# Feed-forward blocks of a two-layer diffusion trunk: every engine in emission order, as a pipeline of seven slots per unit

## The chip, the cores and the metric

The kernel runs on one core of a Trainium2 chip. The metric is the device time of one execution in microseconds (us). The kernel before has a median of 2194.66 us over three runs (2193.26 to 2200.68).

The engines of the core are PE (TensorE: matmuls, and beside them weight loads), DVE (VectorE), ACT (ScalarE), POOL (GpSimd) and SP (SyncE, which here only starts DMA transfers). Each engine executes its own instructions strictly in their order; an instruction that waits holds up all that stand behind it on the same engine.

## The reference, cut to what matters

The trunk has two layers. Each is a mixer (Hyena with mLSTM in layer 0, Mamba-2 in layer 1; neither is touched) and then a SwiGLU feed-forward block:

```python
for l in range(DEPTH):                                  # DEPTH = 2
    ...                                                 # the mixer
    x = x + g1 * out
    h = _rmsnorm(x, P['norm2_g'][l]) * (1 + sc2) + sh2
    ff = (jax.nn.silu(h @ P['ffn_w1'][l]) * (h @ P['ffn_w3'][l])) @ P['ffn_w2'][l]
    x = x + g2 * ff
```

`D_MODEL` is 1024 and the hidden width 2816, which is 22 tiles of 128. There are 640 tokens: 128 of context and 512 latent ones. All is fp32.

## The kernel before, in words

**Precision.** A matrix is split into a high part and the rest, both in the fast fp32 format: ACT copies the value into the rounded type (`split`, L462), and DVE, or POOL where the call says so, subtracts it from the value (L463). A product is three matmuls: high by high, high by low, low by high.

**Seven products.** In the feed-forward block two 128-row blocks of weights and the tokens in two halves of 320 (322 with two columns for shift) are multiplied as a 2x2 block product in the Strassen-Winograd form, with seven products in place of eight. The weights' seven operands are A11, A12 and A22, which are loaded, and S1 to S4, which are sums: S3 and S1 (L1868, L1869), and from these S2 and S4 (L1871, L1872). DVE writes the sums into one PSUM tile, `sw`, which serves both pairs in turn. So a unit's operands are prepared as: A11 and A12 split (`whi`, `wlo`); S3 and S1 formed and split (`wg` or `whif`, `wlof`); S2 and S4 formed over them and split; A22 split with POOL (`whie`, `wloe`).

**Units.** A *hidden tile* is one of the 22 tiles of the hidden width: seven products of 12 matmuls over K = 4 (`hidden`). Its products come into three PSUM banks, ACT copies them out (L1929), DVE adds (L1950, L1960, L1962) and POOL multiplies; ACT takes the SiLU in three pieces (L1970 to L1972) and DVE multiplies (L1973 to L1975). A *pair* is two of the eight tiles of the output, over six hidden tiles: seven products of 9 matmuls over K = 3 (`pair_block`). ACT copies out (L1893), DVE adds (L1907, L1910, L1912), and the result is scaled by the gate and added to `x`: by DVE in one instruction (`residual_part`, L2054), or for one of the four quarters by ACT (scale, L1914) and POOL (add, L1915).

**Order.** A layer's block is hidden tile 0; then three times six hidden tiles and four pairs; tiles 18 to 21 are multiplied by the rest of `w2` plainly (L1670 to L1675). The first hidden tile of the next group stands between a group's own last tile and its pairs. `hidden_quads` writes the hidden tiles, and the sums and splits that the pairs need of them.

**Buffers.** A unit loads two raw tiles of weights (`wraw`, L1422), `r1` with A11 and A12 and `r2` with A22 and the other. There are four buffers, so a unit's two loads wait until the unit two before it has read its own for the last time. `r1` is read last by L1872, `r2` by the split of A22.

**What sets the order on the engines.** The program is built in a context that simulates a timeline (`TileContext(schedule_with_timeline_sim=True)`): a scheduler with modelled durations decides in which order each engine gets its instructions. PE keeps the written order inside a unit.

Of the kernel before, what the change touches and what calls it, by code (L numbers as in the profile page):

```python
# [5 lines left out]
F32 = mybir.dt.float32  # L6
# [5 lines left out]
T = 640  # L12
# [257 lines left out]
class Kern:  # L270
# [1408 lines left out]
    def ffn(self, l, last):  # L1679
# [9 lines left out]
        with self.tc.tile_pool(name=f"hT{l}", **right) as hq, self.tc.tile_pool(name=f"fw{l}", **right) as wq:  # L1689
            with self.tc.tile_pool(name=f"ffn{l}", **right) as fp:  # L1690
                X = self.norm_quads(hq, fp, self.modA[l, 4], self.modA[l, 3], last)
                get2 = self.stream(self.I["w2"][l])
                steps = lambda j: self.hidden(fp, wq, self.I["w13"][l, j], X, j == 0, j % 2, (j + 2) % 3)

                def hid(j):
                    *_, h = steps(j)
                    return h
                h = hid(0)
                for c, (j0, j1) in enumerate(CHUNKS[:3]):
                    U, h = self.hidden_quads(fp, wq, hid, steps, j0, h)  # L1700
                    for e in range(4):
                        self.pair_block(fp, wq, self.I["w2q"][l, c, e], U, e, g2)
                uH, uL = [], []
                for j in range(18, 22):
                    h = h if j == 18 else hid(j)
                    H, L = [self.hb(x, j - 18) for x in "HL"]
                    for i, v in enumerate(h):
                        q = slice(320 * i, 320 * i + 320)
                        self.split(v[:, 2:322], H[:, q], L[:, q])
                    uH.append(H)  # L1710
                    uL.append(L)
# [89 lines left out]
    def hidden_quads(self, p, wq, hid, steps, j, ahead):  # L1801

        U = {}
        N = 320
        pool, sub = self.nc.gpsimd.tensor_tensor, ALU.subtract
        both = lambda v, n: v[:, 0:2 * n].rearrange("p (h n) -> p h n", n=n)[:, :, n - N:n]
        t4 = self.t(p, (128, 2 * N), "t4")

        def put(k, nms, v, dst, i=0):
            n = len(nms)
            dst = [d[:, N * i:N * (i + n)] for d in dst]
            self.split(both(v, 322) if n == 2 else v, *(both(d, N) if n == 2 else d for d in dst))
# [5 lines left out]
        for k in range(3):  # L1820
            a, b = hid(j + 2 * k) if k else ahead
            t1 = a[:, 324:644]
            pool(t1, b[:, 2:322], a[:, 2:322], op=sub)
            f = hb(3 * k) if k < 2 else fs(0)
            put(k, ("B11", "T1"), a, f)
            a2, b2 = hid(j + 2 * k + 1)
            b21, b22, t3, t2 = a2[:, 2:322], b2[:, 2:322], a2[:, 324:644], b2[:, 324:644]
            pool(t3, b22, b[:, 2:322], op=ALU.add)
            if k < 2:
                put(k, ("B21", "T3"), a2, us() if k else hb(1))  # L1830
            else:
                put(k, ("B21",), b21, f, 2)
            pool(t2, b22, t1, op=ALU.add)
            if k < 2:
                put(k, ("B22", "T2"), b2, us() if k else hb(2))
            t5 = t4[:, N * k:N * k + N] if k < 2 else b21
            pool(t5, b21, t2, op=sub)
        after = steps(j + 6)
        next(after)
        f = fs(1)  # L1840
        put(2, ("B22", "T2"), b2, f)
        put(2, ("T3",), t3, f, 2)
        g = [self.t(p, (128, 1024), "wg", WG, F32R) for _ in "HL"]
        self.split(t4, *(v[:, 0:2 * N] for v in g), self.nc.gpsimd)
        self.split(t5, *(v[:, 2 * N:3 * N] for v in g), self.nc.gpsimd)
        for i in range(3):
            U["T4", i] = tuple(v[:, N * i:N * i + N] for v in g)
        return U, next(after)

    def quad_parts(self, src, n, where, e):  # L1850

        nc = self.nc
        vec, sub = nc.vector.tensor_tensor, ALU.subtract
        r1, r2 = [self.raw_unit(src[i], 2 * n) for i in range(2)]
        W = {}

        def put(v, nms, pool, tag, bufs, eng=None):
            w = n * len(nms)
            h, lo = (self.t(pool, (128, 512 * len(nms)), *(("wg", WG) if tag == "g" else ("w" + x + tag, bufs)), F32R)
                     for x in ("hi", "lo"))  # L1860
            self.split(v, h[:, 0:w], lo[:, 0:w], eng)
            for i, nm in enumerate(nms):
                c = slice(n * i, n * i + n)
                W[nm] = h[:, c], lo[:, c]
        v = self.pp.tile([128, 1024], F32, name="sw", tag="sw", bufs=1)[:, 0:2 * n]
        put(r1, ("A11", "A12"), *where[0])
        a, b = slice(0, n), slice(n, 2 * n)
        vec(v[:, a], r2[:, b], r1[:, a], op=sub)  # L1868
        vec(v[:, b], r2[:, b], r2[:, a], op=sub)  # L1869
        put(v, ("S3", "S1"), *where[1])  # L1870
        vec(v[:, a], r1[:, a], v[:, b], op=sub)  # L1871
        vec(v[:, b], r1[:, b], v[:, a], op=sub)  # L1872
        put(v, ("S2", "S4"), *where[2])
        put(r2[:, a], ("A22",), *e, nc.gpsimd)
        return W

    def quad_product(self, W, X, K, i, P, first, ks=None):

        nc = self.nc
        a, b = (("A11", "B11"), ("A12", "B21"), ("S4", "B22"), ("S2", "T2"), ("S3", "T3"), ("S1", "T1"),  # L1880
                ("A22", "T4"))[i]
        for k in ks or range(K):
            h, lo = (v[:, 128 * k:128 * k + 128] for v in W[a])
            xh, xl = X[b, k]
            for j, (w, x) in enumerate(((h, xh), (h, xl), (lo, xh))):
                nc.tensor.matmul(P, w, x, start=first and k == j == 0, stop=k == K - 1 and j == 2,  # L1886
                                 skip_group_check=not first)

    def pair_block(self, p, wq, src, U, e, g):

        nc = self.nc
        n, N = 384, 320
        vec, add, copy = nc.vector.tensor_tensor, ALU.add, lambda o, v: nc.scalar.activation(o, v, AF.Copy)  # L1893
        two = [(p, "g", WG), (wq, "f2", 1)]
        W = self.quad_parts(src, n, ((self.wp, "", 2), two[e % 2], two[1 - e % 2]), (p, "e", 1))
        A, C, D = [self.ps("ab")[:, 0:N] for _ in range(3)]
        c11, c12, c22, _ = [v[:, 322 * i:322 * i + N] for v in [self.t(p, (128, 644), "nt1", 2) for _ in range(2)]
                            for i in range(2)]
        put = lambda i, P, *fl: self.quad_product(W, U, 3, i, P, *fl)
        put(0, A, True)  # L1900
        copy(c11, A)
        put(5, C, True)
        copy(c22, C)
        put(3, A, False)
# [170 lines left out]

# [8 lines left out]
```

## Time and profile before

| | |
|---|---|
| median of three runs | 2194.66 us (2193.26 to 2200.68) |
| the profiled execution: its own time | 2200.58 us |
| its span, first to last instruction | 2198.8 us |
| granted TensorE clock, mean | 0.97 of full speed |
| PE busy | 2056.4 us, 94% of the span |
| DVE busy | 1633.8 us, 74% |
| ACT busy | 1088.4 us, 49% |
| POOL busy | 719.0 us, 33% |

The two feed-forward blocks lie at about 601 to 1024 us and 1732 to 2156 us of the span. PE's busy share is over the whole span; what it leaves idle inside these blocks is read there, from windows and from single instructions.

### The profile page before, as it was taken

What the parts mean: (1) busy time and instruction counts of PE and PEld (TensorE: products, weight loads), DVE (VectorE), ACT (ScalarE), POOL (GpSimd) and SP (SyncE); (2) the same over time, 40 slices, a digit from 0 to 9 for tenths busy, and PEclk for the clock granted to TensorE, in tenths of its full rate; (3) what the DMA queues carried; (4) which work ended last, traced back from release to release, by engine and by line L of the source; (5) the groups of instructions that cost most, each with busy time, mean ns of one, the idle gap of its engine ahead of it and who ended that gap; (6) DMA issues with size and microseconds to landing.
All of it is one profiled execution on the core that took longest, in us unless ns stands there. A gap on an engine that the chain in (4) does not pass through costs nothing.

```text
span 2198.8 us, 35965 instructions
## 1 busy us (share of the span) xinstructions
PE 2056.4 (94%) x14034; PEld 1909.4 (87%) x14034; DVE 1633.8 (74%) x2709; ACT 1088.4 (49%) x1882; POOL 719.0 (33%) x725
## 2 busy tenths in 40 slices
PE   4899999999899999999889999999999899999997
PEld 2788798878799999999889899999988898989996
DVE  7775465678988888887687777776743988888895
ACT  3755634322554545554475556555512554545452
POOL 4311121234444252523332232323312353443422
PEclk9899999989899999999899999999999899999998
DMA  7544431674122222223312222222354122222231
GB/s 280 177 150 158 135 106 64 197 265 156 43 78 66 89 72 82 76 83 118 91 58 67 64 60 71 57 66 62 125 190 145 49 64 81 84 70 87 68 97 48
DMA packets 85638, 225.38 MB, mean 103 GB/s; under 512 B 9979, under 2 KB 27899, under 8 KB 85468
## 3 DMA queue, kind: packets, MB, share of 16 engines
q1 hardware_dynamic: 71756, 205.44, 28.9%
q10 hardware_dynamic: 8960, 9.86, 1.4%
q0 software_dynamic: 4752, 7.79, 1.3%
q8 instruction: 110, 1.80, 0.3%
q14 instruction: 60, 0.49, 0.1%
HBM read 204.86 MB, written 18.36 MB: 102 GB/s over the span
## 4 chain that ended last, share of the span: by engine, by line
PE 68%; DVE 19%; DMA 5%; ACT 3%; issue 3%; POOL 1%; SPq 0%; ACTq 0%; DVEq 0%; POOLq 0%
PE mm L1886 11%; PE aux L1886 9%; PE mm L1670 5%; PE mm L1672 5%; PE mm L1674 5%; PE mm L1671 3%; PE mm L1675 3%; PE mm L1673 3%; DMA wraw<-in_w 2%; DVE x L2054 2%; DVE wlof L463 2%; PE md L1498 2%; DVE wlo L463 1%; PE aux L1319 1%; ACT whi L462 1%
## 5 line engine op out<-in xcount | busy, mean ns | idle before, releaser
L462 ACT ACTIVATE whi<-wraw 128x1024 fp32r<-128x1024 f32 (+1 forms) x176 | 181.2, 1029 | 327.1 <-PE mm L1673 124.9
L1670 PE MATMUL mm<-hH,whi 128*128 128x384 f32 x760 | 267.6, 353 | 0.2 <-DVE x L2054 0.2
L1674 PE MATMUL mm<-hH,wlo 128*128 128x384 f32 x760 | 265.2, 349 | 0.9 <-DVE wlo L463 0.9
L1672 PE MATMUL mm<-hL,whi 128*128 128x384 f32 x760 | 265.0, 349 | 0.5 <-DVE hL L463 0.4
L463 DVE TENSOR_TENSOR wlo<-wraw,whi 128x1024 fp32r<-128x1024 f32 (+1 forms) x162 | 195.0, 1204 | 88.9 <-ACT whi L462 87.2
L1671 PE MATMUL mm<-hH,whi 128*128 128x258 f32 (+1 forms) x568 | 168.6, 297 | 7.4 <-DVE U L639 7.4
L1675 PE MATMUL mm<-hH,wlo 128*128 128x258 f32 (+1 forms) x568 | 167.9, 296 | 0.0
L1673 PE MATMUL mm<-hL,whi 128*128 128x258 f32 (+1 forms) x568 | 167.4, 295 | 0.0
L1670 PEld LDWEIGHTS mm<-hH,whi 128*128 128x128 f32 x760 | 145.0, 191 | 12.6 <-issue 9.3
L1674 PEld LDWEIGHTS mm<-hH,wlo 128*128 128x128 f32 x760 | 144.8, 190 | 5.0 <-issue 3.2
L1672 PEld LDWEIGHTS mm<-hL,whi 128*128 128x128 f32 x760 | 144.9, 191 | 3.8 <-issue 2.0
L1671 PEld LDWEIGHTS mm<-hH,whi 128*128 128x128 f32 x568 | 110.2, 194 | 11.3 <-issue 10.1
L463 POOL TENSOR_TENSOR wloe<-wraw,whie 128x512 fp32r<-128x512 f32 (+1 forms) x68 | 85.1, 1251 | 95.8 <-ACT whie L462 95.8
L1675 PEld LDWEIGHTS mm<-hH,wlo 128*128 128x128 f32 x568 | 109.7, 193 | 4.2 <-issue 3.2
L1673 PEld LDWEIGHTS mm<-hL,whi 128*128 128x128 f32 x568 | 110.2, 194 | 2.3 <-issue 1.3
L463 DVE TENSOR_TENSOR wlof<-sw,whif 128x1024 fp32r<-128x1024 f32 (+1 forms) x68 | 76.5, 1125 | 25.9 <-ACT whif L462 25.9
L1316 POOL TENSOR_TENSOR xw<-xB,ec 128x256 f32<-128x256 f32 x64 | 47.9, 753 | 127.8 <-PE aux L1319 78.3
L462 ACT ACTIVATE wg<-sw 128x1024 fp32r<-128x1024 f32 (+1 forms) x68 | 64.4, 947 | 42.9 <-PE mm L1886 19.5
L1963 POOL TENSOR_TENSOR nt<-nt,rb 128x322 f32<-128x322 f32 x44 | 44.4, 1008 | 125.4 <-DVE nt L1962 113.2
L463 DVE TENSOR_TENSOR wg<-sw,wg 128x1024 fp32r<-128x1024 f32 (+1 forms) x68 | 76.5, 1125 | 10.7 <-ACT wg L462 10.2
L462 ACT ACTIVATE whif<-sw 128x1024 fp32r<-128x1024 f32 (+1 forms) x68 | 64.5, 948 | 33.3 <-DVE sw L1872 29.1
L1366 POOL TENSOR_TENSOR it<-it 128x256 f32<-128x256 f32 x32 | 30.2, 943 | 100.0 <-DVE it L1364 100.0
(793 smaller groups left out, 7063.7 us busy)
## 6 DMA issues: line engine op xcount, KB each, us to landing
wraw<-in_w SPq DMA_DIRECT2D x96, 512.0 KB, 3.5
modr<-in_modw SPq DMA_DIRECT2D x56, 512.0 KB, 4.0
wraw<-in_odw SPq DMA_DIRECT2D x49, 512.0 KB, 3.5
wraw<-in_w2q SPq DMA_DIRECT2D x48, 384.0 KB, 3.1
wraw<-in_evw SPq DMA_DIRECT2D x25, 512.0 KB, 4.3
wraw<-in_modw SPq DMA_DIRECT2D x24, 512.0 KB, 3.8
wraw<-in_odow SPq DMA_DIRECT2D x16, 512.0 KB, 3.7
kd<-kst ACTq DMA_DIRECT2D x16, 256.0 KB, 3.2
```

Of the source, the lines that this page charges most:

```text
L462: self.nc.scalar.activation(h, src, AF.Copy)
L463: (eng or self.nc.vector).tensor_tensor(lo, src, h.bitcast(F32), op=ALU.subtract)
L1316: nc.gpsimd.tensor_tensor(xw, xB[c][:, 0:256].rearrange("p (h e) -> p h e", h=4), self.ec[:, c, hd[d]].unsqueeze(2).to_broadcast([128, 4, ...
L1498: nc.tensor.matmul(ps[32 * j:32 * j + 32, 0:256], self.scond[:, 32 * k:32 * k + 32], rs[0][:, 256 * j:256 * j + 256], start=k == 0, stop=k ...
L1670: nc.tensor.matmul(pA, h, rh[k][:, 0:384], start=f, stop=False)
L1671: nc.tensor.matmul(pB, h, rh[k][:, 384:T_], start=f, stop=False)
L1672: nc.tensor.matmul(pA, h, rl[k][:, 0:384], start=False, stop=False)
L1673: nc.tensor.matmul(pB, h, rl[k][:, 384:T_], start=False, stop=False)
L1674: nc.tensor.matmul(pA, lo, rh[k][:, 0:384], start=False, stop=l)
L1675: nc.tensor.matmul(pB, lo, rh[k][:, 384:T_], start=False, stop=l)
L1886: nc.tensor.matmul(P, w, x, start=first and k == j == 0, stop=k == K - 1 and j == 2, skip_group_check=not first)
L1963: pool(s0, s0, rb1, op=mul)
```

## The change

The seven products, the operands and all arithmetic stay. What changes is the order in which instructions are written, and who decides it:

- `run_units` lists a layer's units and writes them inside `tc.manual_schedule()`, in which every engine gets its instructions in the order in which they are written.
- A unit has seven slots. In slot n stand: its product number n (`SLOTS`, the same order as before); for n < 2 what is left of the unit before (`tail`); the reading of its product n-1 (`read`); steps of the *next* unit's operands (`EARLY` where both are hidden tiles, `LATE` where one is a pair); sums and splits of finished hidden tiles (`hidden_parts`); in slot 1 the split of its own A22; in slot 2 the two loads of the unit after the next.
- The residual addition of the quarter `c12` (`x[2e][:, 320:640]`) is moved from DVE to ACT and POOL, as `c22`'s was: 24 in all (4 pairs by 3 groups by 2 layers). DVE's list shrinks from 2670 to 2646, ACT's grows from 1883 to 1907 and POOL's from 709 to 733.
- Tags change in places: the first hidden tile after pairs has its sums in `f2` and `g` in that order, and a pair's two are swapped.

Its core (what is left out are the removed functions, which are printed above, and `products_first`, the first tile as before):

```diff
+    def run_units(self, l, p, wq, X, g):
...
+        units = [hid(0)]
+        for c in range(3):
+            units += [hid(6 * c + m) for m in range(1, 7)]
+            units += [PairBlock(self, p, wq, I["w2q"][l, c, e], U, e, g) for e in range(4)]
+        units += [hid(j) for j in (19, 20, 21)]
...
+        with self.tc.manual_schedule():
+            for i, u in enumerate(units):
+                prev = units[i - 1] if i else None
+                nxt = units[i + 1] if i + 1 < len(units) else None
+                late = nxt and not (u.hidden and nxt.hidden)
+                extra = self.hidden_parts(p, wq, units, i, U, T4, last)
+                for n, product in enumerate(SLOTS):
+                    if i:
+                        u.product(product)
+                    if n < 2 and prev:
+                        prev.tail(n)
+                    if i and n:
+                        u.read(n - 1)
+                    if nxt:
+                        for step in (EARLY, LATE)[late].get(n, ()):
+                            nxt.prep(step)
+                    for f in extra.get(n, ()):
+                        f()
+                    if i and n == 1:
+                        u.prep_own()
+                    if n == 2 and i + 2 < len(units):
+                        units[i + 2].load()
...
+SLOTS = (0, 5, 3, 2, 4, 1, 6)
+PREP = ("S31", "H31", "L31", "S24", "HA", "LA", "H24", "L24")
+EARLY = {0: ("S31",), 1: ("H31",), 2: ("HA", "L31", "S24"), 3: ("H24", "LA"), 4: ("L24",)}
+LATE = {0: ("S31",), 2: ("HA",), 3: ("LA",), 4: ("H31",), 5: ("L31", "S24"), 6: ("H24", "L24")}
...
+class PairBlock(Unit):
...
+        if n == 0:
...
+            copy(self.c11, self.A)
+        elif n == 1:
+            copy(self.c22, self.C)
+        elif n == 2:
+            copy(self.c12, self.A)
+        elif n in (3, 4):
+            c, d, bank = ((self.c12, 2 * self.e, self.C), (self.c22, 2 * self.e + 1, self.A))[n - 3]
+            vec(c, c, bank, op=ALU.add)
+            copy(c, c, scale=self.g[:, d, 1:2])
+            nc.gpsimd.tensor_tensor(k.x[d][:, N:T], k.x[d][:, N:T], c, op=ALU.add)
+        elif n == 5:
+            vec(self.c11, self.c11, self.D, op=ALU.add)
+            for a, b in ((0, 128), (128, N)):
+                k.residual_part(2 * self.e, self.c11, 0, a, b, self.g)
+    def tail(self, n):
+        if n == 0:
+            for a, b in ((0, 128), (128, self.N)):
+                self.k.residual_part(2 * self.e + 1, self.A, 0, a, b, self.g)
...
+class HiddenTile(Unit):
...
+        if n == 0:
+            self.tiles()
+            copy(self.s0, self.A)
+        elif n == 1:
+            copy(self.c22, self.C)
+        elif n == 2:
+            copy(self.s1, self.A)
...
+    def tail(self, n):
...
+        if n == 0:
+            if not self.first:
+                nc.vector.tensor_tensor(u3, self.A, self.rb1, op=mul)
+            nc.scalar.activation(s0[:, 2:130], s0[:, 2:130], AF.Silu, bias=s0[:, 0:1])
+            nc.scalar.activation(s0[:, 130:], s0[:, 130:], AF.Silu, bias=s0[:, 1:2])
+        else:
+            stt(s0[:, 2:130], u3[:, 2:130], u3[:, 0:1], s0[:, 2:130], op0=add, op1=mul)
+            stt(s0[:, 130:], u3[:, 130:], u3[:, 1:2], s0[:, 130:], op0=add, op1=mul)
```

The names of the steps: S31 forms S3 and S1, S24 forms S2 and S4; H and L are the two halves of a split (ACT copy, DVE subtraction), of A11 and A12 (HA, LA), of S3 and S1 (H31, L31) and of S2 and S4 (H24, L24).

**DVE, inside a group's pairs.** Before, around the end of pair 0; `sw_7279` is the sum tile of pair 1, `wlo_7387` the low part of A11 and A12 of pair 2:

```order
L463 TENSOR_TENSOR wlo_7387<-wraw_7381,whi_7386 128x768
L1907 TENSOR_TENSOR nt1_7197<-nt1_7197,mm_7195 128x320
L2054 SCALAR_TENSOR_TENSOR x0_4575<-nt1_7197,mod0_5_2699,x0_4575 128x320
L463 TENSOR_TENSOR wlof2_7287<-sw_7279,whif2_7286 128x768
L1910 TENSOR_TENSOR nt1_7198<-nt1_7198,aux_7194 128x320
L1912 TENSOR_TENSOR nt1_7303<-nt1_7303,mm_7302 128x320
L1871 TENSOR_TENSOR sw_7279<-wraw_7275,sw_7279 128x384
L2054 SCALAR_TENSOR_TENSOR x2_4577<-nt1_7303,mod0_5_2699,x2_4577 128x128
L2054 SCALAR_TENSOR_TENSOR x2_4577<-nt1_7303,mod0_5_2699,x2_4577 128x192
L1872 TENSOR_TENSOR sw_7279<-wraw_7275,sw_7279 128x384
```

After, during pair 1, which prepares pair 2 (its sum tile is `sw_7315`, its low part of A11 and A12 `wlo_7345`):

```order
L2006 TENSOR_TENSOR sw_7315<-wraw_7242,wraw_7240 128x384
L2007 TENSOR_TENSOR sw_7315<-wraw_7242 128x384
L2020 TENSOR_TENSOR wlo_7345<-wraw_7240,whi_7344 128x768
L2068 TENSOR_TENSOR nt1_7327<-nt1_7327,aux_7302 128x320
L2068 TENSOR_TENSOR nt1_7328<-nt1_7328,mm_7301 128x320
L2020 TENSOR_TENSOR wlof2_7375<-sw_7315,whif2_7374 128x768
L2009 TENSOR_TENSOR sw_7315<-wraw_7240,sw_7315 128x384
L2010 TENSOR_TENSOR sw_7315<-wraw_7240,sw_7315 128x384
L2072 TENSOR_TENSOR nt1_7327<-nt1_7327,mm_7303 128x320
L1974 SCALAR_TENSOR_TENSOR x2_4577<-nt1_7327,mod0_5_2699,x2_4577 128x128
L1974 SCALAR_TENSOR_TENSOR x2_4577<-nt1_7327,mod0_5_2699,x2_4577 128x192
L2020 TENSOR_TENSOR wg_7405<-sw_7315,wg_7404 128x768
```

Before, the split of pair 2's load (`wlo_7387`) stands ahead of the sums S2 and S4 of pair 1 (L1871, L1872). After, all of these rows are of one unit, and the 320-wide residual addition behind the first sum (L2054 on `x0`) is gone.

**ACT, from pair 3 to hidden tile 7.** Before, the same place; `nt1_7624` and `nt1_7625` belong to tile 7, `nt1_7516` to pair 3:

```order
L462 ACTIVATE wg_7610<-sw_7603 128x1024
L1929 ACTIVATE nt1_7624<-aux_7626 128x322
L1914 ACTIVATE nt1_7516<-nt1_7516,mod0_5_2699 128x320
L462 ACTIVATE whif0_7616<-sw_7603 128x1024
L1970 ACTIVATE nt1_7624<-nt1_7624 128x128
L1971 ACTIVATE nt1_7624<-nt1_7624 128x192
L1929 ACTIVATE nt1_7625<-mm_7627 128x322
```

After; `sw_7529` is the sum tile of hidden tile 7, `sw_7639` that of tile 8, `nt1_7654` and `nt1_7655` hold tile 7's products:

```order
L2001 ACTIVATE wg_7618<-sw_7529 128x1024
L2129 ACTIVATE nt1_7654<-aux_7622 128x322
L2001 ACTIVATE wg_7657<-sw_7639 128x1024
L462 ACTIVATE whie_7660<-wraw_7456 128x512
L2129 ACTIVATE nt1_7655<-mm_7623 128x322
L2001 ACTIVATE whi_7677<-wraw_7561 128x1024
L2129 ACTIVATE nt1_7655<-aux_7622 128x322
```

The copy of the second product (`nt1_7655<-mm_7623`) now stands behind the high part of tile 8's S3 and S1 and behind the high part of tile 7's A22.

**PE, at the start of layer 0's block.** Line 1569 spreads the norm's factor over the partitions; it reads `u`, which DVE forms from the norm's sums. Before, two products of hidden tile 0 stand ahead of it (48 matmuls, of which these are the last three):

```order
L1886 MATMUL aux_6369<-hH7_6121,whi_6345 128x322
L1886 MATMUL aux_6369<-hL7_6122,whi_6345 128x322
L1886 MATMUL aux_6369<-hH7_6121,wlo_6346 128x322
L1569 MATMUL mm_6187<-u_6117,ones_86 128x128 x3
L1569 MATMUL mm_6194<-u_6117,ones_86 128x128 x2
```

After, the products that need the norm's last rows stand ahead of it, 24 matmuls:

```order
L2040 MATMUL aux_6233<-hHT3_6140,wg_6210 128x322
L2040 MATMUL aux_6233<-hLT3_6141,wg_6210 128x322
L2040 MATMUL aux_6233<-hHT3_6140,wg_6211 128x322
L1569 MATMUL mm_6187<-u_6117,ones_86 128x128 x3
L1569 MATMUL mm_6194<-u_6117,ones_86 128x128 x2
L2040 MATMUL mm_6228<-hHB0_5832,whi_6216 128x322
```

24 matmuls have gone from ahead of L1569 to behind it in layer 0; in layer 1 it is 12 (36 before, 24 after).

## Rows read from the trace of the kernel before

**Rows 1.** The page: span and instructions.

```profile
span 2198.8 us, 35965 instructions
```

**Rows 2.** Windows: start:end and length, busy by engine (instructions), granted clock, DMA share, GB/s.

```profile
620.00:1000.00 380.00, 361.48 (x2397) 353.94 (x2396) 325.17 (x487) 193.54 (x330) 146.36 (x145) 1.00 0.26 79
1750.00:2130.00 380.00, 362.15 (x2400) 354.59 (x2399) 324.30 (x488) 194.94 (x335) 149.39 (x147) 1.00 0.25 78
640.00:680.00 40.00, 40.00 (x272) 40.00 (x272) 31.60 (x48) 21.54 (x39) 18.17 (x20) 1.00 0.21 70
680.00:758.00 78.00, 71.53 (x472) 69.26 (x472) 67.54 (x102) 37.97 (x64) 27.21 (x26) 1.00 0.25 78
758.00:800.00 42.00, 41.91 (x282) 41.66 (x282) 35.83 (x53) 22.84 (x40) 18.65 (x20) 1.00 0.26 79
```

**Rows 3.** The chain that ended last: start, length, what; hidden products without a gap.

```profile
776.54 1.78 PE mm L1886 x12
```

**Rows 4.** Timeline of PE, one group's waits: start, us, instruction, [idle before <- releaser].

```profile
687.18 0.42 PE L1886 MATMUL mm<-hHT,whif 128*128 128x322 f32 x1 [1.28 <-ACT nt L1929]
691.85 0.41 PE L1886 MATMUL aux<-wlof,whi 128*128 128x320 f32 x1 [1.58 <-DVE wlof L463]
696.55 0.41 PE L1886 MATMUL mm<-hHT,whie 128*128 128x322 f32 x1 [0.58 <-DVE nt L1960]
711.03 0.41 PE L1886 MATMUL mm<-hH,wg 128*128 128x320 f32 x1 [0.56 <-ACT wg L462]
756.99 0.56 PE L1886 MATMUL mm<-hHB,wg 128*128 128x322 f32 x2 [1.24 <-DVE wg L463]
```

**Rows 5.** The chain that ended last, inside a group's pairs.

```profile
830.39 0.48 DVE sw L1872
...
830.89 3.91 DMA wraw<-in_w2q
...
841.44 3.47 DMA wraw<-in_w
```

**Rows 6.** Timeline of DVE inside a group's pairs.

```profile
829.14 1.25 DVE L2054 SCALAR_TENSOR_TENSOR x<-nt,mod,x 128x128 f32<-128x128 f32 x2
...
835.70 0.96 DVE L463 TENSOR_TENSOR wlo<-wraw,whi 128x768 fp32r<-128x768 f32 x1 [1.41 <-ACT whi L462]
836.58 0.48 DVE L1907 TENSOR_TENSOR nt<-nt,aux 128x320 f32<-128x320 f32 x1
837.10 0.55 DVE L2054 SCALAR_TENSOR_TENSOR x<-nt,mod,x 128x320 f32<-128x320 f32 x1
...
841.62 0.67 DVE L2054 SCALAR_TENSOR_TENSOR x<-mm,mod,x 128x128 f32<-128x128 f32 x2 [0.22 <-PE mm L1886]
```

**Rows 7.** Timeline of DVE among hidden tiles.

```profile
628.04 0.69 DVE L1868 TENSOR_TENSOR sw<-wraw 128x512 f32<-128x512 f32 x1
...
637.46 1.21 DVE L463 TENSOR_TENSOR wlof<-sw,whif 128x1024 fp32r<-128x1024 f32 x1
...
639.66 1.12 DVE L1868 TENSOR_TENSOR sw<-wraw 128x512 f32<-128x512 f32 x1 [0.40 <-DMA wraw<-in_w]
```

**Rows 8.** Timeline of ACT among hidden tiles.

```profile
635.00 0.43 ACT L1929 ACTIVATE nt<-mm 128x322 f32<-128x322 f32 x1
635.40 0.63 ACT L462 ACTIVATE whie<-wraw 128x512 fp32r<-128x512 f32 x1
636.04 1.03 ACT L462 ACTIVATE whif<-sw 128x1024 fp32r<-128x1024 f32 x1
```

**Rows 9.** Timeline of POOL, among pairs and among hidden tiles.

```profile
829.04 0.88 POOL L1915 TENSOR_TENSOR x<-x,nt 128x320 f32<-128x320 f32 x1 [6.64 <-ACT nt L1914]
...
640.18 1.21 POOL L1837 TENSOR_TENSOR t<-nt,nt 128x320 f32<-128x320 f32 x1
```

**Rows 10.** Timelines of DVE and PE at the start of layer 0's block.

```profile
608.34 0.89 DVE L1565 TENSOR_TENSOR u<-cst,rsti 128x384 f32<-128x384 f32 x2
...
610.33 1.27 PE L1569 MATMUL mm<-u,ones 128*128 128x128 f32 x10
```

More of the change, by code (lines that the diff above doesn't have):

```diff
@@ L1692, in ffn @@
                 get2 = self.stream(self.I["w2"][l])
[L1693 to L1711, printed above, removed]
+                uH, uL = self.run_units(l, fp, wq, X, g2)
                 if l == 0:
@@ L1806, in hidden_quads, with last_parts, hidden_parts @@
+    def last_parts(self, u):
+        H, L = [self.hb(x, u.j - 18) for x in "HL"]
+        for i, v in enumerate((u.a, u.b)):
+            q = slice(320 * i, 320 * i + 320)
+            self.split(v[:, 2:322], H[:, q], L[:, q])
+        return [(H, L)]
+    def hidden_parts(self, p, wq, units, i, U, T4, last):
+        u, prev = units[i], units[i - 1]
+        if not i or not u.hidden:
+            return {}
         N = 320
-        pool, sub = self.nc.gpsimd.tensor_tensor, ALU.subtract
+        if u.j > 18:
+            t = prev if u.j > 19 else [v for v in units if v.hidden and v.j == 18][0]
+            return {5: [lambda: last.extend(self.last_parts(t))]}
+        pool, sub, add = self.nc.gpsimd.tensor_tensor, ALU.subtract, ALU.add
@@ L1838, in hidden_quads @@
[L1838 to L1887, printed above, removed]
@@ new lines, in hidden_parts, with first @@
+        if m % 2:
+            def first():
+                even.f = hb(3 * k) if k < 2 else fs(0)
+                put(("B11", "T1"), a, even.f)
+            return {2: [lambda: pool(t1, b[:, 2:322], a[:, 2:322], op=sub)], 5: [first]}
+        a2, b2 = prev.a, prev.b
+        b21, b22, t3, t2 = a2[:, 2:322], b2[:, 2:322], a2[:, 324:644], b2[:, 324:644]
+        if k == 0:
+            T4[:] = [self.t(p, (128, 2 * N), "t4")]
+        t5 = T4[0][:, N * k:N * k + N] if k < 2 else b21
+        two, three = lambda: pool(t2, b22, t1, op=add), lambda: pool(t3, b22, b[:, 2:322], op=add)
@@ new lines, in hidden_parts, with mid, rest @@
+        five = lambda: pool(t5, b21, t2, op=sub)
+        if k < 2:
+            return {0: [two], 1: [three], 4: [five],
+                    5: [lambda: put(("B22", "T2"), b2, us() if k else hb(2))],
+                    6: [lambda: put(("B21", "T3"), a2, us() if k else hb(1))]}
+        def mid():
+            five_src = T4[0]
+            T4.append([self.t(p, (128, 1024), "wg", WG, F32R) for _ in "HL"])
+            self.split(five_src, *(v[:, 0:2 * N] for v in T4[1]), self.nc.gpsimd)
+        def rest():
+            f = fs(1)
+            put(("B22", "T2"), b2, f)
+            put(("T3",), t3, f, 2)
@@ L1978, in residual, with end @@
+        def end():
+            self.split(t5, *(v[:, 2 * N:3 * N] for v in T4[1]), self.nc.gpsimd)
+            for i in range(3):
+                U["T4", i] = tuple(v[:, N * i:N * i + N] for v in T4[1])
+        return {0: [two], 1: [three], 2: [mid], 3: [lambda: put(("B21",), b21, even.f, 2)], 4: [five], 5: [rest], 6: [end]}
     def residual(self, d, p, g):
```

247 lines of the change are left out of this document (140 added, 107 removed).

## The prediction, made before the changed kernel had run

> **What bounds the kernel now.** I read the page first: the span is 2198.8 us [rows 1], and the profiled execution took 2200.58 us, 5.9 us above the median of 2194.66 us. All that follows is a difference, so I take it off the median. The change lies in the feed-forward blocks alone, so next come windows. In layer 0's block PE is busy for 361.48 of 380 us, in layer 1's for 362.15 of 380, at full granted clock [rows 2]. PE's busy time overlaps between matmuls, so I count matmuls instead: 12 in a row without a gap take 1.78 us [rows 3], 0.1485 us each. 380 us would hold 2559; there were 2397 and 2400 [rows 2]. The missing 162 and 159 are 24.0 and 23.6 us, together **47.6 us in which PE stood still**. That is all that a better order can give.
>
> Where do they lie? In 640 to 680 us, hidden tiles alone, PE is busy 40.00 of 40 us: nothing is lost there. In 680 to 758 us, which is the border from hidden tiles to pairs, four pairs and the border back, 6.5 us are lost; in the next hidden tiles 0.1 us [rows 2]. So the loss lies at the pairs and their borders. PE's timeline has the single waits of such a group: 1.28, 1.58 and 0.58 us as the pairs begin, 0.56 us inside them (the like three times in the group), 1.24 us where hidden tiles start again [rows 4]. These seven sum to 6.4 us, 38 us in six groups; the other 9 us of the 47.6 go with the same 42 waits, 0.23 us each, as PE starts anew.
>
> DVE and ACT are what PE waits for there, though neither is full: DVE is busy 67.5 of 78 us and ACT 38.0 [rows 2]. It is an order that delays them. Inside the pairs the chain shows it: a load starts when S4 is formed (830.39 + 0.48, load at 830.89), takes 3.91 us, and the next pair's load starts at 841.44 [rows 5]. That is a ring of 10.55 us per pair, where PE needs 63 matmuls, 9.36 us. It closes because DVE has the split of that load ahead of the next S2 and S4: DVE stands still 1.41 us for it at 835.70 [rows 6].
>
> **The change part by part.** A hidden product of 12 matmuls is 1.784 us and a unit 12.5; a pair's product is 1.338 and a unit 9.37 [rows 3]. I place each instruction at its slot, with durations from rows; DVE's and ACT's rows overlap the next by 0.08 us (835.70 + 0.96 against 836.58 [rows 6]), which I take off each.
>
> *Inside pairs.* The split that closed the ring now stands with its own unit, and loads are issued two units ahead in slot 2. The load of `r2` comes free when POOL has split A22, about slot 3; with 3.47 to 3.91 us [rows 5] it lands before slot 0 of the next unit by some 2 us. DVE has about 8.4 us of work in 9.37. The ring goes: all of the 0.56 us waits.
>
> *Hidden to pair.* Sums and splits of the first pair are no longer crowded with those of the last hidden tile, so 1.28, 1.58 and 0.58 go. A new one comes: the pair's first copy is queued on ACT behind two SiLU pieces, which I bound between nothing and their 0.75 us, and take 0.3 us. Six borders: **1.8 us**.
>
> *Pair to hidden.* Here the order costs. Pair 3 prepares a hidden tile, with tiles of 1024 in place of 768. From the end of its fifth product, 6.69 us into the pair, DVE has one chain: add 0.40, L31 1.13, S24 2 x 0.61 (its pieces are as wide as S31's), add 0.40, two residual pieces 1.17, L24 1.13 [rows 6, 7]; it ends at 12.1, which is 2.8 us into the hidden unit. Then two residual pieces 0.59 and S31 of the next tile 2 x 0.61, to 4.6; on ACT the high part of that 0.95, the high part of A22 0.55, and the copy of the second product 0.43 [rows 8], to 6.5. The copies are queued behind both, and PE needs the bank at slot 3, 5.35 us. That is 1.2 us late, and up to 2.0 with both pieces of S31 under a POOL add (1.12 for 0.69 each [rows 7]); I take 1.3, since POOL has little to do there. Six borders: **7.8 us**, in place of 6 x 1.24.
>
> *Hidden tiles* stay dense in the sum. The same chain there starts at the unit's beginning: u3 0.40, S31 1.22, high part 0.95, A22 0.55, copy 0.43, with the ACT pieces before them ready; it ends at about 4.4 us against 5.35, 0.95 us to spare.
>
> *Start.* 24 matmuls less stand ahead of L1569 in layer 0. `u` is ready at 608.34 + 0.89 = 609.2, and L1569 ran at 610.33 [rows 10], 1.1 us later. So 24 x 0.1485 = 3.6 us less cover cost 3.6 - 1.1 = 2.5 us. Layer 1 has 12 less, 1.8 us; with the same 1.1 us to spare that is 0.7. **3.2 us**, bounds 0 and 5.4.
>
> *End.* 24 fewer of the plain matmuls are mixed with the last tile's work (21 in place of 45): bound 0 and 3.6 us, I take **0.5** since most of that work is ready by then.
>
> *The moved addition.* 24 times DVE saves 0.55 us (837.10 [rows 6]), and ACT gains a scale (about a copy of that width, 0.43 us [rows 8]) and POOL an add of 0.88 us [rows 9]. ACT and POOL are busy 38.0 and 27.2 us of 78 in that stretch [rows 2], so it costs nothing on PE's path. Without that idle time it would be 24 x 0.88 = 21 us. It can cost through DVE: two pieces of the residual that read `x` and a tile took 1.25 us at 829.14, while POOL's add ran from 829.04; two that read PSUM and `x` took 0.67 us, with POOL idle, at 841.62 [rows 6, 9]. S31, which has both inputs in SBUF, took 1.12 us under a POOL add at 640.18 and 0.69 us alone [rows 7, 9]. The Trainium skill, "SBUF — State Buffer", section "Who interferes with whom", states that DVE with two SBUF inputs and GpSimd share a port pair as an exclusive lock, so that the later one stands still for the other's whole instruction; these rows agree in direction, but the delay they show is 0.4 to 0.6 us. By the rule 24 adds could hold up DVE for 21 us, by the rows for 24 x 0.58 = 14; both are time of an engine that is idle 10.5 of 78 us, so the sum takes neither, and the case where it tells is a rival below.
>
> **Sum.** 47.6 - 1.8 - 7.8 - 3.2 - 0.5 = 34.3 us. 2194.66 - 34.3 = **2160 us**, 1.6% faster (for the profiled execution 2166). Its own range is 2153 to 2170, from the bounds of the start, the end and the borders.
>
> **The rivals.**
>
> *No wait at the borders.* If DVE reaches S31 early enough, 1.8 + 7.8 come back: 2151 us. For it: 0.58 us of the chain is contention, and 0.5 us more of slack in the order would nearly do. Against it: every step of the chain has a row. Chance 0.12.
>
> *The borders keep their old waits.* Then 1.28 + 1.58 + 0.58 + 1.24 = 4.7 us [rows 4] and 4 x 0.23 remain in each of six groups, 33.6 us, and only the inner ones go: 47.6 - 33.6 - 3.7 (start and end) = 10.3 us, 2184 us. For it: one sum tile in PSUM and the same buffers serve as before. Against it: 1.58 was a wait for a split that DVE did late behind other units' work. Chance 0.16.
>
> *Slower: hidden tiles become late.* Before, they were dense, with an order that could put a copy ahead. Now ACT must pass the high parts of the next S31 and of A22 before it copies the second product. 42 units have this chain with 0.95 us to spare. S31 collides with POOL's add of the finished tile, which the new order puts into the same slot: 1.12 in place of 0.69 twice makes +0.86 us, which just fits. If DVE also comes to the unit late by 1 us, because work of the slots before queues behind waits for PE, each unit loses about 1 us. The gain is gone from 34.3 / 42 = 0.82 us per unit, so from DVE 1.8 us late; slower by the bound below from 0.98. At 1.2 us it is 50 us: 2210 us. By the rule of the Trainium skill's page named above ("SBUF — State Buffer") this chain would be later than the rows make it: with adds of 0.88 and 1.21 us in its way it would be 1.1 us past its spare time of 0.95 at worst, an estimate of 48 us in 42 units. Chance 0.12, since DVE is busy only 31.6 of 40 us [rows 2] and so has time to catch up in each unit.
>
> *It changes nothing.* The lists of all engines do differ; 0.04 is for losses that happen to cancel the gain.
>
> **How the numbers follow.** The forecast has 0.56, its neighbours at 2151 and 2184 have 0.12 and 0.16. The range reaches over all three, 2146 to 2187, and leaves out 0.16. The three runs of before lie 0.34% apart, so about 0.3% (6.6 us) is what this measurement can tell from no change: faster 0.84, same 0.04, slower 0.12.
>
> **What would show it.** In the same windows PE should do about 2510 to 2540 matmuls in 380 us; more than 2550 would show the rival without border waits, under 2460 the old waits. In pairs, loads should start every 9.4 us, not 10.55, and DVE should not wait at its split of A11 and A12. PE should wait about 1.3 us, for an ACT copy, once per return to hidden tiles, in the fourth slot of the first hidden unit; and about 2 us at L1569 in layer 0. PE waiting on that copy in *every* hidden unit would prove the slower rival. Wrong would be, too, a DVE that is over 95% busy between 640 and 680 us.

## The result

The changed kernel takes 2161.26 us (median of 2158.82, 2161.26 and 2167.08), beside 2194.66 before; one execution of each that took about twice as long (4988.62 and 3952.47 us) is left out. The ratio is 0.9846, 95% interval 0.9804 to 0.9888. Measured again it took 2163.67 us, beside 2196.3: ratio 0.9852 (0.9835 to 0.9869). That is some 33 us faster, where 2160 was forecast within 2146 to 2187.

The page of the changed kernel, its span (as [rows 1]) and engines:

```profile
span 2157.0 us, 35915 instructions
PE 2044.5 (95%) x14034; PEld 1909.8 (89%) x14034; DVE 1601.8 (74%) x2685; ACT 1098.0 (51%) x1906; POOL 732.6 (34%) x749
```

Its windows, as [rows 2]: 380 us of either block, hidden tiles alone, the four pairs of a group, the return to hidden tiles:

```profile
611.00:991.00 380.00, 372.93 (x2491) 371.19 (x2490) 315.70 (x485) 205.19 (x356) 158.25 (x161) 0.99 0.27 84
1727.00:2107.00 380.00, 372.88 (x2494) 371.15 (x2493) 319.85 (x488) 207.08 (x358) 158.75 (x161) 0.99 0.26 83
640.00:680.00 40.00, 40.00 (x272) 40.00 (x271) 31.08 (x47) 22.11 (x38) 20.91 (x21) 1.00 0.26 79
684.00:722.00 38.00, 37.72 (x257) 37.46 (x256) 33.44 (x56) 20.28 (x37) 12.43 (x14) 1.00 0.30 97
722.00:740.00 18.00, 15.93 (x108) 15.61 (x107) 15.84 (x25) 9.53 (x16) 6.77 (x7) 1.00 0.26 88
```

94 matmuls more fit into the same 380 us in each block, 14 us of PE; 2491 and 2494 are under the 2510 to 2540 that I had named, and over the 2460 of the old waits. Hidden tiles were full and still are; the pairs lose 0.3 of 38 us; what is left is lost at one place, the return to hidden tiles (2.1 of 18 us). The list of PE's waits (waiter, awaited, us in all, times, longest) has only two lines of these blocks, and the timeline shows one of each kind, two in a group, where before there were six or seven:

```profile
PE mm L2040 <- ACT nt L2129: 12.5, 6, 2.1
PE aux L2040 <- ACT nt L2056: 1.7, 6, 0.3
```

```profile
686.60 0.41 PE L2040 MATMUL aux<-hH,wg 128*128 128x320 f32 x1 [0.28 <-ACT nt L2056]
728.66 0.41 PE L2040 MATMUL mm<-hH,wg 128*128 128x322 f32 x1 [2.07 <-ACT nt L2129]
```

In the chain, which ran through loads every 10.55 us [rows 5], the pairs now repeat from S3 to S3 on DVE, without a load in between:

```profile
696.14 1.18 DVE sw L2006
...
705.43 1.15 DVE sw L2006
...
714.66 1.26 DVE sw L2006
```

That is 9.29 and 9.23 us a pair, near PE's own pace (63 matmuls at 0.1485 us are 9.36). The wait of 2.07 us is longer than the 1.3 foreseen. ACT and DVE in the last pair show why:

```profile
718.21 0.57 ACT L2056 ACTIVATE nt<-nt,mod 128x320 f32<-128x320 f32 x1 [1.82 <-DVE nt L2068]
718.68 1.01 ACT L2001 ACTIVATE whif<-sw 128x1024 fp32r<-128x1024 f32 x1
...
726.74 1.02 ACT L2001 ACTIVATE wg<-sw 128x1024 fp32r<-128x1024 f32 x1 [2.88 <-DVE sw L2007]
727.66 0.62 ACT L462 ACTIVATE whie<-wraw 128x512 fp32r<-128x512 f32 x1
728.18 0.43 ACT L2129 ACTIVATE nt<-mm 128x322 f32<-128x322 f32 x1
```

```profile
717.70 0.48 DVE L2068 TENSOR_TENSOR nt<-nt,aux 128x320 f32<-128x320 f32 x1
718.59 0.49 DVE L2068 TENSOR_TENSOR nt<-nt,mm 128x320 f32<-128x320 f32 x1 [0.41 <-PE mm L2040]
719.72 1.23 DVE L2020 TENSOR_TENSOR wlof<-sw,whif 128x1024 fp32r<-128x1024 f32 x1 [0.65 <-ACT whif L2001]
```

The copy for which PE waits (728.18) does stand behind the two high parts, as foreseen. But the chain that delays them begins earlier than I had it: the moved addition's scale (718.21) waits for DVE's sum of `c12`, the high part of S3 and S1 (718.68) is queued behind it though its input had long been there, and DVE waits 0.65 us for that. And the waits have a second price. These are windows of 4 us behind the six of them (the number behind the five engines is the granted clock):

```profile
728.66:732.66 4.00, 4.00 (x27) 4.00 (x28) 3.93 (x6) 2.88 (x4) 2.44 (x3) 1.00 0.33 126
843.24:847.24 4.00, 4.00 (x16) 4.00 (x17) 3.43 (x6) 2.88 (x4) 1.86 (x2) 0.57 0.40 131
959.42:963.42 4.00, 4.00 (x16) 4.00 (x17) 3.34 (x6) 2.97 (x5) 1.04 (x1) 0.57 0.40 128
1844.84:1848.84 4.00, 4.00 (x27) 4.00 (x28) 3.93 (x6) 2.88 (x4) 2.44 (x3) 1.00 0.39 128
1959.34:1963.34 4.00, 4.00 (x16) 4.00 (x17) 3.47 (x6) 2.88 (x4) 1.89 (x3) 0.57 0.38 130
2075.38:2079.38 4.00, 4.00 (x16) 4.00 (x17) 3.49 (x6) 2.96 (x5) 1.08 (x2) 0.57 0.45 131
```

Behind four of the six the clock is at its lower level (1.2 GHz) for most of the window, and 16 matmuls run where 27 do at the higher one: 11 x 0.1485 = 1.6 us each, 6.5 us in all.

One sum over the timelines tells where the gain lies. From the first to the last product of the two blocks I add up the time from each matmul's start to the next one's, less 0.1485 us each; what is left, PE's loss, was 53.1 us before and is 24.9 us in the change: 28.2 us less. It is 24.9 in the second profile of the change too.

### The profile page after: what moved, and what is told of

Read it like the earlier page. It is cut to its first block, busy times and chain, and to the rows that moved or that the text cites. A ratio compares the mean times of both kernels' runs of the same rounds, so it can differ in the third digit from the quotient of the medians.

```text
span 2157.0 us, 35915 instructions
## 1 busy us (share of the span) xinstructions
PE 2044.5 (95%) x14034; PEld 1909.8 (89%) x14034; DVE 1601.8 (74%) x2685; ACT 1098.0 (51%) x1906; POOL 732.6 (34%) x749
## 4 chain that ended last, share of the span: by engine, by line
PE 75%; DVE 15%; ACT 3%; issue 3%; DMA 2%; POOL 1%; DVEq 0%; SPq 0%; ACTq 0%; POOLq 0%
PE aux L2040 14%; PE mm L2040 13%; PE mm L1670 5%; PE mm L1672 5%; PE mm L1674 5%; PE mm L1671 3%; PE mm L1675 3%; PE mm L1673 3%; PE md L1498 2%; DVE x L1974 2%; PE aux L1319 1%; PE aux L1361 1%; PE aux L1340 1%; DVE wlof L2020 1%; DVE sw L2006 1%
## 5 line engine op out<-in xcount | busy, mean ns | idle before, releaser
L462 ACT ACTIVATE whi<-wraw 128x1024 fp32r<-128x1024 f32 x108 | 114.4, 1059 | 225.5 <-PE mm L1673 121.7
L463 DVE TENSOR_TENSOR wlo<-wraw,whi 128x1024 fp32r<-128x1024 f32 x94 | 119.4, 1270 | 55.3 <-ACT whi L462 54.6
L1316 POOL TENSOR_TENSOR xw<-xB,ec 128x256 f32<-128x256 f32 x64 | 47.6, 747 | 128.3 <-PE aux L1319 78.2
L2020 DVE TENSOR_TENSOR wlo<-wraw,whi 128x1024 fp32r<-128x1024 f32 (+1 forms) x68 | 76.8, 1129 | 15.5 <-ACT whi L2001 15.5
L2160 ACT ACTIVATE nt<-nt 128x128 f32<-128x128 f32 x44 | 17.8, 405 | 112.0 <-POOL nt L2145 107.8
```

Source lines behind the costliest of these rows:

```text
L462: self.nc.scalar.activation(h, src, AF.Copy)
L463: (eng or self.nc.vector).tensor_tensor(lo, src, h.bitcast(F32), op=ALU.subtract)
L1316: nc.gpsimd.tensor_tensor(xw, xB[c][:, 0:256].rearrange("p (h e) -> p h e", h=4), self.ec[:, c, hd[d]].unsqueeze(2).to_broadcast([128, 4, ...
L2020: vec(lo, r1 if step == "LA" else self.v, h.bitcast(F32), op=sub)
```

## The experiments

Theory **order**: before, DVE and ACT had other units' work ahead of what PE needed next, and the hand-set order gives that time back. Its first rival, **relief**: the time comes from the 24 x 0.55 us that the moved addition takes off DVE. All ratios are to the kernel before, measured beside each run (2195.94 to 2197.06 us).

**The addition back on DVE.** In the pair's reading of `c12`:

```diff
             vec(c, c, bank, op=ALU.add)
+            if n == 3:
+                k.residual_part(d, c, N, N, T, self.g)
+                return
             copy(c, c, scale=self.g[:, d, 1:2])
```

> The changed kernel with the residual addition of c12 back on DVE, as one 320-wide instruction right behind c12's sum; all orders else as in the change. Theory 'order' (the gain comes from PE no longer waiting at pairs and borders): the time stays near the changed kernel's 2164 us, if anything below it: ACT's scale of c12 (0.57 us, behind the sum) no longer holds up the high part of S3 and S1 on ACT, so PE's wait where hidden tiles start again should fall from 2.07 to about 1.3 us, 6 x 0.75 = 4.5 us, to 2158 to 2164. Rival 'relief' (the gain comes from 24 x 0.55 us taken off DVE): 13 us or more are lost, 2175 to 2180.

2152.29 us, ratio 0.9796 (0.9781 to 0.9810): faster than the change by 11 us, beyond what either theory said. PE's waits:

```profile
PE mm L2040 <- ACT nt L2132: 8.5, 6, 1.5
PE aux L2040 <- ACT nt L2056: 1.7, 6, 0.3
```

The six waits are 1.40 us, as forecast, 4 us less in all. Most of the rest is the clock: it stays at the higher level behind all six. PE's loss in the blocks is 14.4 us, 10.5 less than in the change. So where the change puts it, the moved addition is a loss.

**The addition alone, in the old order.** In `pair_block`:

```diff
-        self.residual_part(2 * e, c12, N, N, T, g)
+        nc.scalar.activation(c12, c12, AF.Copy, scale=g[:, 2 * e, 1:2])
+        nc.gpsimd.tensor_tensor(self.x[2 * e][:, N:T], self.x[2 * e][:, N:T], c12, op=add)
```

> The kernel before with the moved addition alone: ACT scales c12 and POOL adds it, the scheduler orders everything as before. Theory 'order': DVE is 0.55 us a pair freer, but the ring through the load stays; 0 to 5 us faster than before (ratio 0.998 to 1.000), and PE's waits on splits and copies at L1886 stay near 18 us a layer. Rival 'relief': 15 to 33 us faster, ratio 0.985 to 0.993.

2179.68 us, ratio 0.9917 (0.9898 to 0.9937): 17 us faster. Here *relief* was right, and I had it wrong. What is left of PE's waits (before, the list had two lines more: 6.5 us in 12 waits for `wg` and 3.5 us in 6 for `whif`, those inside the pairs):

```profile
PE aux L1886 <- DVE wlof L463: 9.8, 6, 2.0
PE mm L1886 <- ACT nt L1930: 6.9, 6, 1.3
PE mm L1886 <- DVE wg L463: 4.5, 4, 1.2
PE mm L1886 <- DVE nt L1961: 3.5, 6, 0.6
```

The waits inside the pairs are gone, all those at the borders stay. The ring through the load broke without the hand-set order. The chain of the kernel before shows what the addition did there. In the first pairs of four of the six groups it has no load in it; from PE's product to PE's wait it runs over DVE and one ACT copy, and the addition that was moved is one of its pieces:

```profile
705.29 0.50 DVE nt L1907
...
705.82 0.55 DVE x L2054
...
709.66 0.48 DVE sw L1872
...
710.16 0.82 ACT wg L462
...
711.03 0.56 PE mm L1886 x2
```

The waits inside the pairs were 0.51 to 0.72 us, most of them 0.56, and the piece that went is 0.55 us. That fits, but the scheduler also ordered the rest anew, and the two were not told apart.

**The new text, ordered by the scheduler.**

```diff
-        with self.tc.manual_schedule():
+        if True:
```

> The changed kernel's text without the hand-set order: the same units, tags, loads and moved addition, but the scheduler decides the engines' order again. Theory 'order' in its narrow form (it is the hand-set order that counts): the waits at pairs come back, 2185 to 2200 us. Rival 'text' (what counts is how the units are written, with loads two units ahead and the operands in steps): 2155 to 2170 us, and in pairs a load starts every 9.3 to 9.4 us.

2169.07 us, ratio 0.987 (0.9854 to 0.9887). The narrow *order* is wrong: there is no wait inside the pairs. The time is at the slow end of what *text* gave, but the borders wait as they did before (8.7 us in 6 waits for a split, 7.4 in 6 for a copy, 4.6 in 4 for `wg`), which *text* did not say. So the scheduler's order costs at the borders, not inside the pairs. Between this run and the change only the hand-set order differs: it takes away these 20.7 us of waits and brings the change's 14.2 us and 6.5 us of low clock. PE's loss in the blocks is 28.1 us here and 24.9 there, and the two intervals of the ratio overlap: as first written, the hand-set order gained little. Against the addition-alone run 10 us are gone; of its waits the six for DVE's `nt` (3.5 us) are no longer there, and which part of the text gives the rest stays open.

**The copy first at the return.** In the hidden unit behind pairs, with its own table (`border` is that unit):

```diff
+FIRST = {0: ("S31",), 2: ("H31", "L31", "S24"), 3: ("HA", "H24", "LA"), 4: ("L24",)}
...
+                    if border and n == 3:
+                        u.prep_own()
```

> The changed kernel, but in the hidden unit that follows pairs ACT copies the second product before it takes the high part of the next S3 and S1, and takes the high part of its own A22 after the third copy. Theory (the 2.07 us wait is the copy queued on ACT behind these two, which come late because DVE's S3 and S1 come late): PE's wait for an ACT copy of a hidden product falls from 12.5 us in six waits to under 2, and the time by 11 to 14 us against the changed kernel, ratio to before 0.978 to 0.981. Rival (the border is late by DVE's work, so the wait only moves to the next operand or copy): the wait returns at a later product, the gain is under 4 us.

2153.22 us, ratio 0.9801 (0.9786 to 0.9816). The time fell by 10 us, more than the rival allowed, and yet its account of the wait is right:

```profile
PE aux L2044 <- DVE nt L2145: 10.4, 6, 1.7
PE aux L2044 <- ACT nt L2060: 1.7, 6, 0.3
```

The wait has moved to the seventh product, behind DVE's sum of `c22`, and is only 2 us less. The rest is the clock again: behind waits of 1.73 us it did not fall once.

**The high part ahead of the reading.** With the addition left on ACT and POOL; only, in slot 4 of a unit that prepares with `LATE`, the high part of S3 and S1 comes first:

```diff
+                    if late and n == 4:
+                        nxt.prep("H31")
                     if i and n:
                         u.read(n - 1)
...
```

(The entry for slot 4 in `LATE` goes.)

> The changed kernel, with the moved addition kept on ACT and POOL; only, in a unit before or behind which a pair stands, ACT takes the high part of S3 and S1 before slot 4's reading (the sum of c12 and its scale), not behind it. Theory 'queue' (the moved addition costs time because its scale on ACT waits for DVE's sum of c12 and holds up the high part behind it): PE's six waits for an ACT copy where hidden tiles start again fall from 2.07 to about 1.4 us, the granted clock no longer falls to 0.5 behind them, and the time is 2150 to 2156, as with the addition back on DVE. Rival 'port' (what costs is POOL's 24 more additions, during which DVE's instructions with two inputs in SBUF take longer): the waits stay at 1.8 us or more, the time at 2159 to 2165.

2149.83 us, ratio 0.9789 (0.9774 to 0.9803). Theory *queue* holds: the waits are 1.41 us, the clock stays at the higher level behind all six, and the time is 0.2 us under the lower end of its range:

```profile
PE mm L2042 <- ACT nt L2131: 8.4, 6, 1.4
PE aux L2042 <- ACT nt L2058: 1.7, 6, 0.3
```

```profile
720.40 1.03 ACT L2003 ACTIVATE whif<-sw 128x1024 fp32r<-128x1024 f32 x1 [0.79 <-PE aux L2042]
721.33 0.55 ACT L2058 ACTIVATE nt<-nt,mod 128x320 f32<-128x320 f32 x1
```

The high part now runs ahead of the scale. PE's loss in the blocks is 14.3 us, as with the addition back on DVE (14.4): one line's place on ACT is worth 10.5 us of it (14 us by the medians), and POOL's additions, which are all still there, cost nothing that shows.

**A split on POOL.** The low part of A11 and A12 of the hidden tile behind pairs is subtracted by POOL:

```diff
+            eng = nc.gpsimd if step == "LA" and self.hidden and self.j % 6 == 1 and self.j > 1 else nc.vector
...
```

> The changed kernel, but the low part of A11 and A12 of the hidden tile behind pairs is subtracted by POOL, not DVE (six instructions of some 1.2 us on DVE). Theory 'DVE chain' (the border is late by the sum of DVE's work in the last pair): the chain to S3 and S1 of the next tile is some 1.1 us earlier, the six waits fall from 2.07 to about 1 us, no clock at 0.5 behind them, 2148 to 2153 us. Rival (the chain starts at the product or at ACT's queue behind this split, so that it has slack): waits above 1.8 us, 2159 to 2165.

2157.5 us, ratio 0.9823 (0.9809 to 0.9838), waits of 1.82 us: the rival is right, though the time is a little under its range. DVE is 1.2 us freer ahead of the sum of `c12`, but waits for PE there (0.72 us) and then still for ACT's high part (0.33 us). Some 3 us of the 6 gained are the clock, which fell behind two of the six waits only.

**Two doses for the spare time of hidden tiles.** My rival on the slower side rested on 0.95 us by which the copy of the second product is early. First the high part of A11 and A12 in slot 1, ahead of that copy; then that high part copied twice (the second writes the same values):

```diff
-EARLY = {0: ("S31",), 1: ("H31",), 2: ("HA", "L31", "S24"), 3: ("H24", "LA"), 4: ("L24",)}
+EARLY = {0: ("S31",), 1: ("H31", "HA"), 2: ("L31", "S24"), 3: ("H24", "LA"), 4: ("L24",)}
```

> The changed kernel with a dose: in units before a hidden tile ACT takes the high part of A11 and A12 (about 0.95 us) in slot 1, ahead of the copy of the second product, not behind it. Theory 'margin 0.95' (in hidden tiles that copy ends 0.95 us before PE needs the bank): the 28 inner units wait 0 to 0.1 us, the 6 border units 1 us more than 2.07, behind all of them the clock falls; 2168 to 2178 us. Rival 'wide margin' would show no more than the border's part, under 2170 with the inner ones at nothing; rival 'no margin' 1 us in each of 34 units, 2195 us or more.

> As the dose before, with that high part copied twice (the second copy writes the same values): two copies, 1.9 us, ahead of the copy of the second product. Theory 'margin 0.95': 28 inner units wait about 0.95 us each and PE starts anew 0.23 us later each time, the 6 border units 2 us more: 28 x 1.2 + 12 + 3 = 49 us, 2205 to 2220 us. If the clock falls to 0.5 behind waits of 1 us too, 28 x 1.7 us more, about 2260. Rival 'wide margin': the inner units still do not wait, under 2185 us.

2175.51 us (ratio 0.9904, 0.9887 to 0.9921) and 2216.27 us (1.0091, 1.0076 to 1.0106). With one dose eight waits for that copy, six of 3.0 us at the borders, where the clock fell behind four (I had said all), and two of 0.17 us; with two:

```profile
PE mm L2042 <- ACT nt L2131: 39.2, 20, 4.1
PE aux L2042 <- ACT nt L2131: 11.3, 14, 0.8
```

34 waits: six of 4.1 us at the borders, 28 of 0.8 to 1.1 us in the inner units. With 1.9 us put ahead, the spare time is thus 0.8 to 1.1 us. PE's loss is 49 us more than in the change, as the expectation's sum had it. So the slower rival's price per unit is right; its condition was not met.

**The change once more**, for a comparison:

> The changed kernel once more, for a comparison on the same chip: ratio to before 0.984 to 0.986, six waits of 2.07 us where hidden tiles start again, and the granted clock at 0.5 for 3.4 us behind some of them (4 of 6 in the first profile).

2163.67 us, with the same waits (12.4 us in six) and the clock down behind the same four.

**The border's order** (the border run). On top of the high part ahead: DVE forms the next S3 and S1 ahead of the last pair's residual pieces, the copy first, the low part of A11 and A12 late:

```diff
+                    if border and n == 0:
+                        nxt.prep("S31")
...
+FIRST = {2: ("H31", "L31", "S24"), 3: ("HA", "H24"), 4: ("L24",), 5: ("LA",)}
```

> The high part of S3 and S1 ahead of slot 4's reading, as in the run before with that edit (1.4 us left at each return to hidden tiles), and in the hidden unit behind pairs: DVE forms the next S3 and S1 ahead of the last pair's two residual pieces (0.58 us earlier); ACT copies the second product before the high part of the next S3 and S1; the low part of A11 and A12 goes behind the sum of c22. Theory 'order at the border': the six waits of 1.4 us fall to 0.5 or less, no clock at 0.5, 6 x 1.1 = 7 us less than that run's 2150: 2140 to 2145 us, ratio to before 0.974 to 0.977. Rival 'DVE's work' (the border is full, the wait only moves on to a later product, as with the copy alone): 2147 us or more.

2153.15 us, ratio 0.9804 (0.979 to 0.9819): no gain over the high part ahead alone, so rival *DVE's work* is right. 7.1 us of wait had moved to the seventh product. Then the low part of S2 and S4 behind the sum, the run named sum first (`3: ("HA", "H24"), 5: ("LA", "L24")`):

> As the border run, in which the six waits had moved to the seventh product, 7.1 us behind DVE's sum of c22, which DVE reached only after the low part of S2 and S4 (1.2 us, itself 0.7 us late); now that low part goes behind the sum, in slot 5 after the low part of A11 and A12. Theory 'order at the border': the sum comes 1.2 to 1.4 us earlier, all waits at the return to hidden tiles together fall from 8.4 to under 2 us, 2141 to 2147 us, ratio to before 0.974 to 0.978. Rival 'DVE's work' (the border's work does not fit whatever its order): the wait moves into the next hidden unit, the sum of waits stays at 6 us or more, 2149 us or more.

2149.32 us, ratio 0.9783 (0.9768 to 0.9797): above the forecast range. Of 8.4 us of waits at the return 2.7 are left, now in the next hidden unit: by the waits that is nearer to *order at the border*, while the time is that of the high part ahead alone within the intervals. In the profiles PE's loss in the blocks falls from 14.3 (the high part ahead) to 10.9 us, which the medians are too coarse to show. Last, the pair's first copy ahead of the SiLU pieces:

```diff
+                    swap = i and not u.hidden and prev.hidden
+                    if swap and n == 0:
+                        u.read(0)
...
```

(The later reading of that product is left out there.)

> As the run named sum first, and where pairs begin ACT copies the pair's first product ahead of the last hidden tile's two SiLU pieces, not behind them. Theory (the six waits of 0.28 us there are that copy queued behind SiLU pieces that wait for POOL): they go, 1.7 us of wait and 6 x 0.1 to 0.2 us of starting anew: 2 to 3 us less than the run named sum first. Rival (the SiLU pieces, 0.34 us later, hold up DVE's sums for the pair): the waits return at another place and the time is the same or longer.

2145.4 us, ratio 0.9767 (0.9753 to 0.9782), 4 us less than the run named sum first. The theory is right: the six waits of 0.28 us are gone and none came in their place; PE's loss is 7.5 us, 3.4 less. The two blocks are nearly full:

```profile
PE mm L2049 <- ACT nt L2138: 2.2, 4, 0.6
PE mm L2049 <- DVE nt L2150: 0.5, 1, 0.5
```

```profile
612.00:992.00 380.00, 378.61 (x2555) 376.99 (x2554) 325.33 (x498) 210.65 (x366) 171.95 (x168) 1.00 0.27 85
1720.00:2100.00 380.00, 378.27 (x2545) 376.41 (x2544) 327.64 (x498) 211.33 (x364) 170.52 (x163) 1.00 0.26 83
```

This version beats both kernels: 51 us under before, 18 under the change.

## Why the prediction was right, step by step

- **Where the time is**: right for 28 us of the gain, which was PE standing still at pairs and borders. The list of single waits was not quite right. Four of the six groups have a wait where hidden tiles start again, not six ([rows 4] show the first), so that the groups have 40 waits of 35 us together, not 42 of 38.
- **Inside pairs**: right in effect, the ring is gone. As for its cause I had only the order and the load (the load at 841.44 in [rows 5] is a hidden tile's, `in_w`); the addition alone takes the waits away too, and in the first pairs of four groups the chain before has no load.
- **Hidden to pair**: right. 0.28 us six times, 1.7 us against 1.8, and the copy behind the SiLU pieces is shown to be the cause by the last run. That the hand-set order took the old waits away there is shown by the run of the same text ordered by the scheduler, which has most of them (8.7 and 7.4 us).
- **Pair to hidden**: right in mechanism (a copy queued on ACT behind two high parts that DVE made late), mis-sized: 7.8 us forecast, 12.5 us of waits and 6.5 us of low clock measured. I began the chain with DVE's sum and low part at the end of the fifth product and took the high part for ready. With it really ready, in the run that puts it ahead, the wait is 1.4 us, as against the 1.3 of the sum.
- **The moved addition at nothing**: this step failed. I looked whether ACT and POOL had idle time, and they do. But ACT's scale waits for a sum, and what stands behind it waits too: 10.5 us of PE's loss, by the run that puts the addition back and by the run that puts the high part ahead alike. The delay between DVE and POOL decided nothing here, since the run that puts the high part ahead keeps all of POOL's additions. And I had set its size, 0.4 to 0.6 us, against the other's whole time; what counts is how much of the other is left when the sum begins. S3 at 714.58 took 1.33 us beside POOL's split of 714.35, which ran 1.01 us; its neighbour at 715.95, with POOL idle, took 0.70. In the change 20 such sums of 512 columns began while POOL was at work, and each ended 0.55 to 0.56 us after POOL did; three began first and took their 0.69 us. (So the 1.12 us of [rows 7] came from the POOL instruction ahead of the add at 640.18, which began after the sum.) The Trainium skill, "SBUF — State Buffer", section "Who interferes with whom", states that a DVE instruction with two SBUF inputs contends with a GpSimd instruction that reads SBUF, that the shared ports are an exclusive lock, and that the order of issue decides who is blocked. The trace agrees, in these 23 cases.
- **Hidden tiles dense, 0.95 us to spare**: right, by the windows and by the two doses. The rival counted 42 units with this chain; there are 34 (28 inner ones and six at borders), so its bounds per unit were too low.
- **Start, 3.2 us**: wrong. PE did not wait at L1569 in either block. I had held `u` at its old time; counted from the block's first product it was ready 1.9 us earlier in layer 0 and 0.5 us in layer 1.
- **End, 0.5 us**: wrong in sign. Behind the blocks' last products stand 45 plain matmuls more than before (24 and 21), 6.7 us of PE's work. Yet the stretch from there to the next norm's L1569 in layer 0 and to the end of the span in layer 1 grew by 0.7 us in all. 3.6 us of the difference are shorter waits of PE there (8.3 to 6.5 us in layer 0, 8.5 to 6.7 in layer 1); why they fell, and the rest of it, was not traced.
- **The sum**: 34.3 against 33, in good part by luck. Inside the blocks the terms gave 47.6 - 1.8 - 7.8 - 3.2 = 34.8 us, and PE's loss fell by 28.2: the border and its clock cost 11 us more than I took, the start cost 3.2 us less, and PE had some more to give back. The 6.0 us behind the blocks (6.7 - 0.7), which I had as a cost of 0.5, made up for it: 34.2 us in the profiles. The two spans differ by 41.8 us; the rest lies ahead of the first block (8.5 us, where two profiles of the changed kernel differ by 5.4 us from each other) and between the two (0.9 us the other way).

## What to carry to other kernels

An engine with idle time is not free for an instruction that waits: what counts is what stands behind it in the queue, so a moved instruction goes behind everything that is ready earlier. After a change of order, look at the places where one kind of work gives way to another; there the waits that are left collect, and one removed shows up at the next product until the engine that is really late has less to do. And change one thing at a time: here the change without the moved addition gains 45 us, the moved addition alone 17, both together 33.

## What the runs showed of the hardware

How TensorE's clock follows short waits was not in any sum of the prediction. I took windows of 4 us behind each of the six waits and counted those whose granted clock was under 0.7: waits of 1.4 us 0 of 6, of 1.73 us 0, of 1.82 us 2, of 2.07 us 4 (the same four in both runs), of 3.0 us 4, of 4.1 us 6. (One wait of 1.96 us in the kernel before did not bring it down either.) PE had run without a wait for some 40 us ahead of each. So waits that differ by 0.3 us can differ by 1.6 us more in price, and why some waits of one length bring the clock down and others not was not settled.
